# A hybrid recurrence and sparse-attention block: operands of the matrix multiplications moved by 64 bytes in on-chip memory

## The chip, the cores and the metric

The kernel runs on one core of one Trainium2 chip. The time is that of the whole program on the device, in microseconds (us). Before the change three runs took 1340.19, 1340.39 and 1341.03 us; the median, 1340.39 us, is the time that the change is measured against.

TensorE (PE in the profile) multiplies matrices. Each of its products has two operands in the on-chip memory SBUF: a *stationary* one of 128 x 128 elements, which a weight load (PEld, LDWEIGHTS) brings into the array, and a *moving* one of 128 rows and 128 to 512 columns, which then streams through it. Results go to PSUM. VectorE (DVE) and ScalarE (ACT) work on tiles, GpSimd (POOL) does little here, and SyncE (SP) issues nearly all the transfers.

## What is computed

One layer over 512 tokens of width 2048, in float32: a normalisation, one wide projection `w_in`, two branches (a gated linear recurrence, and sparse attention for which an indexer picks the keys), a gated merge, an output projection `w_out`, a residual sum and a last normalisation.

```python
h = rmsnorm(x, norm_w[layer])
proj = h @ w_in[layer]
...
q_idx = (cq @ w_qidx).reshape(b_, s_, IDX_HEADS, IDX_DIM)
kv = (rmsnorm(c_kv, kv_norm_w) @ w_ukv).reshape(b_, s_, B_HEADS, 2 * B_HEAD_DIM)
...
rel_scores = jax.nn.relu(jnp.einsum('bthd,bsd->bths', qi_blk.astype(F32), k_idx))
...
merged = (jax.nn.sigmoid(m_a) * (y_a @ w_pa[layer])
          + jax.nn.sigmoid(m_b) * (y_b @ w_pb[layer]))
x = x + merged @ w_out[layer]
return rmsnorm(x, final_norm_w)
```

## The kernel before

**Three products for one.** A float32 operand is split into a high part that the fast format `fp32r` holds exactly and a low rest (`split`, line 70). `mm3` (line 74) multiplies high by high, high by low and low by high; its three matmuls are lines 75, 76 and 77 of the profile. In the profile's names, `pp<-sh,wh` is a matmul into the PSUM tile `pp` with the moving operand `sh` and the stationary operand `wh`.

**Jobs.** The program is a list of jobs that are run in order. Each takes weights from device memory through two buffers (`load`), has ACT and DVE split them (`prep`, three pieces ahead), and multiplies. Other work (normalisations, the recurrence, attention) is cut into steps, one of which is issued between pieces of a job (`pump`). The order of every engine's instructions is written out this way; no scheduler moves them.

**Units of seven products.** For the gates and for most of the output projection, 2 x 2 blocks of matrices are multiplied with seven block products in place of eight (`pair_unit`, line 1141; `PRODUCTS`, line 1131). A unit has eight *chunks* k = 0 to 7, one for 256 rows of the contracted side; a chunk is 7 products x 2 halves x 3 matmuls = 42 matmuls, each with a moving operand of 256 columns. Thirteen units belong to `w_in` (eleven of `gate_pair` and two more; the moving operand is x: the tiles `xh`, `xl`, and its block sums `sh0` to `sh7` and `sl0` to `sl7`; the stationary one is the weights: `bh`, `bl` as loaded and `wh`, `wl` for the sums that `pair_sums` makes of them). Three more belong to `w_out` (`out_job`, line 1407), where the sides are exchanged: the weights move, and the merged activations (`mh`, `ml`, `so`) are stationary.

**Where operands lie.** Tiles are placed by pools in the order in which they are asked for, so a tile's byte address is settled by what was allocated ahead of it. Here only the address modulo 128 is of interest, called the *residue* below; the operands that this change touches lie at residue 0 or 64. The kernel sets it in several places by spare elements of 4 bytes: `weight_places` (line 136) takes 64 elements more than it needs and starts at `at`; `STILL` and `RANK` are 16 elements, `MOVED` is 48, so all three mean residue 64 and `at` = 0 means residue 0. `pair_specs` (line 1133) has an argument `even`: in the chunk whose number it is, `pair_sums` puts its sums at residue 0 instead of at `R.at`, residue 64.

What the built program places, by the residue of its tiles:

| operands (moving / stationary) | before | after |
|---|---|---|
| units of `w_in`: x and its sums / weights and their sums | 0 / 64, but 64 / 64 for the sums of chunk 2 | 0 / 64, but 0 / 0 for the sums of chunk 2 of the first unit |
| units of `w_out`: weights and their sums / activations | 64 / 0, but 0 / 0 for the sums of chunk 2 of each unit | 64 / 0, but 0 / 0 for the sums of chunk 0 of the first unit |
| index jobs, `w_qidx`, 384 columns: normalised `cqh`, `cql` / weights | 64 / 0 | 64 / 0 in the even jobs, 64 / 64 in the odd ones |
| index scores, 512, 384 and 256 columns: keys `kih`, `kil` / queries `qih`, `qil` | 64 / 64 | 64 / 0 |
| `w_ukv` jobs 1 and 3, keys part, 512 columns: `ckh`, `ckl` / weights | 0 / 0 | 0 / 64 |
| `w_ukv` jobs 1 and 3, values part, 256 columns: weights / `ckh`, `ckl` | 0 / 0 | 64 / 0 |

**Around the index.** Eight jobs over `w_qidx` (line 1238) make the queries of two of the 16 heads each; `qidx_evac` splits them into `qih` and `qil`, and `idx_gen` (line 610) multiplies them with the keys in three sizes and adds what comes out into the score `M`. Its tile `relu` has two buffers and lies above the queries in a pool that grows downwards, so that eight elements more in each of them put the queries 64 bytes lower. Four jobs `ukv_job` (line 932) make keys and values for two heads each.

Of the kernel before, what the change touches and what calls it, by code (L numbers as in the profile page):

```python
# [26 lines left out]
F32 = mybir.dt.float32  # L27
# [8 lines left out]
NK = D // 128  # L36
# [7 lines left out]
STILL, MOVED, RANK = 16, 48, 16  # L44

EVEN = 2
# [4 lines left out]
def hybrid_block(ctx, tc, x, w_in, w_uq, w_qidx, w_ukv, w_pa, w_pb, w_out, rel_bias, final_norm_w,  # L51
# [4 lines left out]
    w_in, w_uq, w_qidx, w_ukv = w_in[0], w_uq[0], w_qidx[0], w_ukv[0]  # L56
    w_pa, w_pb, w_out = w_pa[0], w_pb[0], w_out[0]
# [21 lines left out]
    def mm(ps, l, r, first, last):  # L79
        PE.matmul(ps, l, r, start=first, stop=last, skip_group_check=True)  # L80
# [4 lines left out]
    cols = const.tile([128, 32], F32, name="cols")  # L85
# [11 lines left out]
    gate_d = dram.tile([48, 128, T], F32, name="gate_d")  # L97
# [18 lines left out]
    R = SimpleNamespace(load=0.0)  # L116


    specs = []
# [139 lines left out]
    def start():  # L259
        R.v0 = enter("v0")  # L260
        R.x = enter("sums")
        p0 = enter("p0", side="right")
        R.xt = []
        for k in range(8):
            if k in (EVEN, EVEN + 1):
                R.x.tile([128, STILL if k == EVEN else 64 - STILL], F32, name=f"gap{k}")
            R.xt.append(R.x.tile([128, 2, T], F32, name=f"xt{k}", tag=f"sh{k}"))
            if k < 6:
                xs_l.append(R.x.tile([128, 4, 256], FR, name=f"sl{k}", tag=f"sl{k}"))
            else:  # L270
                R.dg = R.x.tile([128, 1024], F32, name=f"dg{k}", tag=f"sl{k}")
                if k == 6:
                    R.row, R.total = R.dg[:, 0:T], R.dg[:, T:]
        R.rinv = cols[:, 25:29]
        ident = R.dg[:, 0:128]
        parts = ((0, 2), (2, 4), (4, 8), (8, 12), (12, 16))
        wh, wl, wr = [], [], []
        sums = p0.tile([128, 2, T], F32, name="sums")

        def load_x(k, i=None):  # L280
            n = slice(0, 2) if i is None else slice(i, i + 1)
            SP.dma_start(R.xt[k][:, n, :], x_t[:, 2 * k + n.start:2 * k + n.stop, :])

        def load_w(c):
            k0, k1 = parts[c]
            wr.append(p0.tile([128, 4, 272], F32, name="fr", bufs=3))
            SP.dma_start(wr[c][:, 0:k1 - k0, :], w_first[:, k0:k1, :])

        A.dma_start(wc, w_norm)
        load_x(0, 0)  # L290
        load_w(0)
        load_x(0, 1)
        load_w(1)
        load_x(1)
        A.dma_start(ident, c_ident)
        A.dma_start(cols[:, 0:25], w_cols)

        def load_group(c):
            load_x(2 * c - 2)
            load_w(c)  # L300
            load_x(2 * c - 1)

        load_group(2)
        heat_src = p0.tile([128, 128], F32, name="rows")
        G.memset(heat_src, 1.0)
        G.tensor_copy(ones_r, heat_src)
        A.activation(R.rinv[:, 0:1], eps, AF.Sqrt)
        warm = mmp.tile([128, T], F32, name="acc")
        for _ in range(8):
            PE.matmul(warm[:, 0:128], ones, ones, start=True, stop=True)  # L310
        pools4 = [(mmp, "acc"), (sdp, "sd")] * 2
        accs = [pool.tile([128, T], F32, name="pf", tag=tag)[:, 0:272] for pool, tag in pools4]
        squares = {}

        def square(k):
            squares[k] = p0.tile([128, 2, T], F32, name="sq", bufs=3)
            A.activation(squares[k], R.xt[k], AF.Square)

        def add(k):
            if k:  # L320
                V.tensor_tensor(sums, squares.pop(0) if k == 1 else sums, squares.pop(k), op=OP.add)

        def three(c, n):
            k0, k1 = parts[c]
            xp, wp = ((xh, wh), (xl, wh), (xh, wl))[n]
            for k in range(k0, k1):
                for t in range(4):
                    mm(accs[t], xp[k // 4][:, k % 4, t * 128:t * 128 + 128], wp[c][:, k - k0, :],
                       k + n == 0, k == NK - 1 and n == 2)

        behind = ()
        for c, (k0, k1) in enumerate(parts):
            n = slice(0, k1 - k0)
            wh.append(p0.tile([128, 4, 272], FR, name="fh", bufs=3))
            wl.append(p0.tile([128, 4, 272], FR, name="fl", bufs=3))
            G.tensor_copy(wh[c][:, n], wr[c][:, n])
            for k in range(k0, k1):
                src = R.xt[k // 2][:, k % 2, :]
                hi, lo = xh[k // 4][:, k % 4, :], xl[k // 4][:, k % 4, :]
                A.activation(hi, src, AF.Copy, scale=wc[:, k:k + 1])  # L340
                V.scalar_tensor_tensor(lo, src, wc[:, k:k + 1], hi.bitcast(F32), op0=OP.mult, op1=OP.subtract)
            V.tensor_tensor(wl[c][:, n], wr[c][:, n], wh[c][:, n].bitcast(F32), op=OP.subtract)
            if c < 2:
                load_group(c + 3)
            if c == 2:
                load_ahead()
            if c == 4:
                prep(0, 1)
            pairs = range(k0 // 2, k1 // 2)
            for k in behind:  # L350
                square(k)
            for k in behind if c < 4 else ():
                add(k)
            if c == 4:
                last = behind
            behind = pairs
            for n in range(3):
                three(c, n)
        prep(0, 2)
        for k in last:  # L360
            add(k)
        for k in behind:
            square(k)
            add(k)
        V.tensor_tensor(R.total, sums[:, 0, :], sums[:, 1, :], op=OP.add)
        R.first = accs
        leave("p0")
# [232 lines left out]
    def qidx_evac(h0):  # L600
        def evac(c, ps):
            qh = R.q.tile([128, 384], FR, name="qih", bufs=3)
            ql = R.q.tile([128, 384], FR, name="qil", bufs=3)
            split(qh, ql, ps)
            if len(waiting) > 1:
                lanes["misc"].append(waiting.pop(0))
            waiting.append(idx_gen(h0 + c, qh, ql))
        return evac

    def idx_gen(h, qh, ql):  # L610
        place = {b: bank("sc")[:, 0:b * 128 + 128] for b in (3, 2, 1)}
        for b in (3, 2, 1):
            s = slice(b * 128 - 128, b * 128)
            n = slice(0, b * 128 + 128)
            mm3(place[b], qh[:, s], ql[:, s], R.kih[:, n], R.kil[:, n], True, True)
        r = R.q.tile([128, 1280], F32, name="relu", bufs=2)
        for b in (3, 2, 1):
            m = slice(MO[b], MO[b] + b * 128 + 128)
            A.activation(r[:, m], place[b], AF.Relu, scale=IDX_SCALE)
        for b in (3, 2, 1):  # L620
            m = slice(MO[b], MO[b] + b * 128 + 128)
            w = widx[:, b, h:h + 1]
            if h == 0:
                V.tensor_scalar(R.M[:, m], r[:, m], w, None, op0=OP.mult)
            else:
                V.scalar_tensor_tensor(R.M[:, m], r[:, m], w, R.M[:, m], op0=OP.mult, op1=OP.add)
        yield
# [303 lines left out]

    def ukv_job(p):
        at = len(specs)
        specs.append(([(0, 512, w_ukv[0:256, p * 512:(p + 1) * 512])], 2, 512))

        def run():
            drain("att")
# [195 lines left out]
    def pair_specs(src, cols, n, even=-1):  # L1133

        for k in range(n):
            parts = [(i * 256, i * 256 + 256, src[k * 256:(k + 1) * 256, c:c + 256]) for i, c in enumerate(cols)]
            if cols[1] == cols[0] + 256:
                parts = [(0, 512, src[k * 256:(k + 1) * 256, cols[0]:cols[0] + 512])]
            specs.append((parts, 2, 512, "pair", k == even))
# [18 lines left out]
            if k in ahead:  # L1158
                ahead[k]()

    def pair_job(src, cols, n, rhs, evac):
        at = len(specs)
        pair_specs(src, cols, n)
        jobs.append(lambda: pair_unit(at, n, rhs, evac))

    def pair_evac(dst, fn):
# [19 lines left out]
    def gate_pair(j):  # L1186
        fn = AF.Silu if j < 16 else AF.Sigmoid
        pair_job(w_in, [GATE_COL[j], GATE_COL[j] + 256], NK // 2, x_pair,
                 pair_evac([gate_d[j:j + 2], gate_d[j + 2:j + 4]], [fn, fn]))


    GATE_COL = [3072 + j * 128 for j in range(8)] + [5008 + j * 128 for j in range(8)]
# [44 lines left out]
    jobs.append(open_branches)  # L1237
    for p in range(8):
        feat_job(w_qidx, p * 256, 2, 4, 4, lambda k: (R.cqh[:, k, 128:], R.cql[:, k, 128:]),
                 qidx_evac(2 * p), width=384)  # L1240

    def end_index():
        lanes["misc"].extend(waiting)
# [163 lines left out]
    def out_job():  # L1407
        at = len(specs)
        for cb in range(3):
            pair_specs(w_out, [cb * 512, cb * 512 + 256], NK // 2, even=EVEN)  # L1410
        for i in range(8):
            specs.append(([(0, 512, w_out[i * 256:(i + 1) * 256, 1536:])], 2, 512)
                         + ((f"so{i}",) if i >= 4 else ()))
# [217 lines left out]
```

## Time and profile before

| | before |
|---|---|
| median of three runs | 1340.39 us |
| the profiled execution, first to last instruction | 1338.4 us |
| what a run's time has beside that span | 2.0 us |
| PE, busy share of the span | 99% |
| DVE, busy share | 80% |
| ACT, busy share | 50% |
| mean granted PE clock | 0.998 |
| the sixteen units of seven products, matmuls in the trace | 5376 of 10876 |

The time of the profiled execution is known as its span; the 2.0 us is the difference of the runs' median from it. A matmul's row in the profile shows some 0.28 us for 256 columns and 0.39 us for 512, while the next one starts after 0.11 and 0.23 us: matmuls are pipelined, and what one costs is the time from its start to the next one's start. The timeline gives starts to 0.01 us; over many matmuls in a row their count gives the mean to a fraction of a nanosecond.

### The profile page before, as it was taken

The page shows a single profiled execution, that of the slowest core. Times are in us where ns is not written, and L with a number is a line of the kernel's source. Part 1 is how long each engine was busy: PE and PEld are TensorE (multiplying, and loading weights), DVE is VectorE, ACT ScalarE, POOL GpSimd, SP SyncE. Part 2 cuts the span into 40 slices and gives each one's busy share as a digit, 9 for nine tenths or more (in the row PEclk, how much of TensorE's full clock was granted, in tenths as well). Part 3 has the DMA queues.
Part 4 walks back from the last instruction along what each step waited for, and adds up shares of the span by engine and source line. Part 5 has one row for each costly group of instructions (what it writes and reads, how often), then busy time and mean ns, then how long its engine had stood idle before and what let it go on. Part 6 is the DMA issues. An engine that isn't in the chain of part 4 may idle for free.

```text
span 1338.4 us, 26561 instructions
## 1 busy us (share of the span) xinstructions
PE 1327.9 (99%) x10876; PEld 1236.6 (92%) x10876; DVE 1068.6 (80%) x1705; ACT 666.8 (50%) x1060; POOL 39.0 (3%) x54
## 2 busy tenths in 40 slices
PE   9999999999999999999999999999999999999997
PEld 8988999999999999999999888888888888899996
DVE  7777889998888888886778988875656658899856
ACT  6455555454454444443666465656434423444435
POOL 2000000000000000000000000020001000000000
PEclk9999999999999999999999999999999999999999
DMA  6343545543454444434523525445655556653454
GB/s 243 93 112 113 155 142 158 148 141 107 143 158 143 142 143 142 128 113 159 181 85 110 182 73 158 127 149 178 242 193 189 186 177 220 201 162 123 168 202 166
DMA packets 141290, 205.82 MB, mean 154 GB/s; under 512 B 8672, under 2 KB 82032, under 8 KB 141040
## 3 DMA queue, kind: packets, MB, share of 16 engines
q1 hardware_dynamic: 140592, 203.78, 48.3%
q8 instruction: 85, 1.39, 0.4%
q10 hardware_dynamic: 576, 0.35, 0.1%
q14 instruction: 37, 0.30, 0.1%
HBM read 168.42 MB, written 35.68 MB: 152 GB/s over the span
## 4 chain that ended last, share of the span: by engine, by line
PE 96%; DMA 1%; DVE 1%; ACT 1%; SPq 0%; issue 0%; ACTq 0%; DVEq 0%
PE pp L75 15%; PE pp L77 15%; PE pp L76 15%; PE acc L75 14%; PE acc L76 14%; PE acc L77 14%; PE hl L80 1%; PE ho L80 1%; DMA wr<-in_w_in_dram 1%; PE sc L75 1%; PE sc L76 1%; PE sc L77 1%; DMA xt<-in_x_t_dram 0%; PE hp L80 0%; PE po L77 0%; PE po L76 0%
## 5 line engine op out<-in xcount | busy, mean ns | idle before, releaser
L150 ACT ACTIVATE bh<-wr 128x768 fp32r<-128x768 f32 x128 | 108.2, 845 | 215.3 <-issue 99.7
L152 ACT ACTIVATE wh<-sv 128x512 fp32r<-128x512 f32 x256 | 152.3, 623 | 84.4 <-DVE sv L145 66.9
L75 PE MATMUL pp<-sh,wh 128*128 128x256 f32 x624 | 172.7, 277 | 0.0
L77 PE MATMUL pp<-sh,wl 128*128 128x256 f32 x624 | 172.7, 277 | 0.0
L76 PE MATMUL pp<-sl,wh 128*128 128x256 f32 x624 | 172.6, 277 | 0.0
L72 DVE TENSOR_TENSOR wl<-wr,wh 128x1024 fp32r<-128x1024 f32 (+1 forms) x104 | 125.6, 1209 | 56.7 <-ACT wh L71 56.7
L154 DVE TENSOR_TENSOR wl<-sv,wh 128x1024 fp32r<-128x1024 f32 x128 | 156.5, 1222 | 6.1
L153 DVE TENSOR_TENSOR bl<-wr,bh 128x768 fp32r<-128x768 f32 x128 | 122.2, 955 | 46.9 <-ACT bh L150 46.2
L71 ACT ACTIVATE wh<-wr 128x1024 fp32r<-128x1024 f32 (+1 forms) x104 | 108.2, 1040 | 92.2 <-PE acc L76 44.1
L75 PE MATMUL acc<-xh,wh 128*128 128x512 f32 x304 | 120.3, 396 | 0.0
L76 PE MATMUL acc<-xl,wh 128*128 128x512 f32 x304 | 118.5, 390 | 0.0
L77 PE MATMUL acc<-xh,wl 128*128 128x512 f32 x304 | 118.5, 390 | 0.0
L76 PEld LDWEIGHTS pp<-sl,wh 128*128 128x128 f32 x624 | 117.3, 188 | 0.0
L75 PEld LDWEIGHTS pp<-sh,wh 128*128 128x128 f32 x624 | 117.3, 188 | 0.0
L77 PEld LDWEIGHTS pp<-sh,wl 128*128 128x128 f32 x624 | 117.3, 188 | 0.0
L75 PE MATMUL pp<-xh,bh 128*128 128x256 f32 x416 | 114.8, 276 | 0.0
L77 PE MATMUL pp<-xh,bl 128*128 128x256 f32 x416 | 114.8, 276 | 0.0
L76 PE MATMUL pp<-xl,bh 128*128 128x256 f32 x416 | 114.8, 276 | 0.0
L75 PE MATMUL acc<-yh,wh 128*128 128x512 f32 x256 | 100.3, 392 | 0.0
L76 PE MATMUL acc<-yl,wh 128*128 128x512 f32 x256 | 99.7, 390 | 0.0
L77 PE MATMUL acc<-yh,wl 128*128 128x512 f32 x256 | 99.7, 389 | 0.0
L145 DVE TENSOR_TENSOR sv<-wr 128x512 f32<-128x512 f32 x128 | 87.9, 686 | 7.2 <-DMA wr<-in_w_in_dram 4.4
(390 smaller groups left out, 3608.4 us busy)
## 6 DMA issues: line engine op xcount, KB each, us to landing
wr<-in_w_in_dram SPq DMA_DIRECT2D x136, 512.0 KB, 3.8
wr<-in_w_out_dram SPq DMA_DIRECT2D x32, 512.0 KB, 3.8
mg<-gate_d SPq DMA_DIRECT2D x48, 256.0 KB, 4.2
gate_d<-c SPq DMA_DIRECT2D x44, 256.0 KB, 4.9
wr<-in_w_in_dram SPq DMA_DIRECT2D x36, 256.0 KB, 3.0
wr<-in_w_pa_dram SPq DMA_DIRECT2D x16, 512.0 KB, 4.3
wr<-in_w_pb_dram SPq DMA_DIRECT2D x16, 512.0 KB, 4.1
wr<-in_w_qidx_dram SPq DMA_DIRECT2D x8, 512.0 KB, 4.1
```

The source lines that it names most:

```text
L71: A.activation(hi, src, AF.Copy)
L72: V.tensor_tensor(lo, src, hi.bitcast(F32), op=OP.subtract)
L75: PE.matmul(ps, lh, rh, start=first, stop=False, skip_group_check=True)
L76: PE.matmul(ps, lh, rl, start=False, stop=False, skip_group_check=True)
L77: PE.matmul(ps, ll, rh, start=False, stop=last, skip_group_check=True)
L80: PE.matmul(ps, l, r, start=first, stop=last, skip_group_check=True)
L145: V.tensor_tensor(sv[:, 0:2, :], b[:, 1:3, :], b[:, 0:1, :].to_broadcast([128, 2, 256]), op=OP.add)
L150: A.activation(bh, b[:, 1:4, :], AF.Copy)
L152: A.activation(vh[:, i:i + 2, :], sv[:, i:i + 2, :], AF.Copy)
L153: V.tensor_tensor(bl, b[:, 1:4, :], bh.bitcast(F32), op=OP.subtract)
L154: V.tensor_tensor(vl, sv, vh.bitcast(F32), op=OP.subtract)
```

## The change

Four edits, none of which adds, removes or reorders an instruction: on each engine the instructions stand as they stood, apart from the numbers of buffers and lines.

- `start` no longer allocates two gaps of 16 and 48 elements before the tiles `xt2` and `xt3` (whose places the sums `sh2`, `sl2` and `sh3` take later), so that all of x's sums lie at residue 0.
- The argument `even`, which puts the weight sums of one chunk at residue 0, is given to the first unit of `w_in` alone (chunk 2), and of `w_out` to the first unit alone, where it is now chunk 0.
- The tile `relu` is 1288 elements wide in place of 1280.
- The odd jobs of `w_ukv` and of `w_qidx` have their weights at residue 64 instead of 0.

```diff
@@ start
         for k in range(8):
-            if k in (EVEN, EVEN + 1):
-                R.x.tile([128, STILL if k == EVEN else 64 - STILL], F32, name=f"gap{k}")
             R.xt.append(R.x.tile([128, 2, T], F32, name=f"xt{k}", tag=f"sh{k}"))
@@ idx_gen
-        r = R.q.tile([128, 1280], F32, name="relu", bufs=2)
+        r = R.q.tile([128, 1288], F32, name="relu", bufs=2)
@@ ukv_job
-        specs.append(([(0, 512, w_ukv[0:256, p * 512:(p + 1) * 512])], 2, 512))
+        specs.append(([(0, 512, w_ukv[0:256, p * 512:(p + 1) * 512])], 2, 512, RANK if p % 2 else 0))
@@ pair_job
-    def pair_job(src, cols, n, rhs, evac):
+    def pair_job(src, cols, n, rhs, evac, even=-1):
         at = len(specs)
-        pair_specs(src, cols, n)
+        pair_specs(src, cols, n, even)
@@ gate_pair
-                 pair_evac([gate_d[j:j + 2], gate_d[j + 2:j + 4]], [fn, fn]))
+                 pair_evac([gate_d[j:j + 2], gate_d[j + 2:j + 4]], [fn, fn]), even=EVEN if j == 0 else -1)
@@ the eight index jobs
         feat_job(w_qidx, p * 256, 2, 4, 4, lambda k: (R.cqh[:, k, 128:], R.cql[:, k, 128:]),
-                 qidx_evac(2 * p), width=384)
+                 qidx_evac(2 * p), width=384, place=RANK if p % 2 else 0)
@@ out_job
-            pair_specs(w_out, [cb * 512, cb * 512 + 256], NK // 2, even=EVEN)
+            pair_specs(w_out, [cb * 512, cb * 512 + 256], NK // 2, even=-1 if cb else 0)
```

## The prediction

> **What bounds the kernel now.** I read the page first (busy times, the granted clock in slices, the chain of work that ended last), then the list of all that PE waited for.
>
> ```profile
> PE 1327.9 (99%) x10876; PEld 1236.6 (92%) x10876; DVE 1068.6 (80%) x1705; ACT 666.8 (50%) x1060; POOL 39.0 (3%) x54
> PEclk9999999999999999999999999999999999999999
> PE 96%; DMA 1%; DVE 1%; ACT 1%; SPq 0%; issue 0%; ACTq 0%; DVEq 0%
> PE acc L310 <- POOL ones_r L306: 1.4, 1, 1.4
> PE pf L80 <- ACT xh L340: 0.6, 1, 0.6
> PE pf L80 <- POOL fh L336: 0.3, 1, 0.3
> PE pf L80 <- DVE fl L342: 0.3, 1, 0.3
> ```
>
> PE is the bound, at full clock, and waits 2.6 us in all, at the very start. So the time can only fall if matmuls start closer to each other, and a nanosecond per matmul is worth about 11 us over the 10876. Busy time says nothing on that, since rows overlap; I therefore took starts from the timeline of PE. The first matmul (L75) of a chunk is easy to find, and a chunk is 42 matmuls. In the sixth of the `w_in` units, chunk 2, chunk 3 and chunk 4 begin at the first three rows here, and chunk 2 of the next unit at the fourth:
>
> ```profile
> 334.22 0.28 PE L75 MATMUL pp<-xh,bh 128*128 128x256 f32 x1
> 339.14 0.28 PE L75 MATMUL pp<-xh,bh 128*128 128x256 f32 x1
> 343.90 0.28 PE L75 MATMUL pp<-xh,bh 128*128 128x256 f32 x1
> 372.46 0.28 PE L75 MATMUL pp<-xh,bh 128*128 128x256 f32 x1
> ```
>
> Chunk 2 takes 4.92 us, chunk 3 takes 4.76, and the six chunks from 343.90 on take 28.56, again 4.76 each: 113.3 ns per matmul. Chunk 2 is the one in which x's sums share residue 64 with the weights. What would meet there is shown by two more rows:
>
> ```profile
> 145.44 0.28 PE L75 MATMUL pp<-sh,wh 128*128 128x256 f32 x1
> 145.44 0.19 PEld L76 LDWEIGHTS pp<-sl,wh 128*128 128x128 f32 x1
> ```
>
> The weight load for the next matmul begins with the matmul itself, so one stationary and one moving operand are read from SBUF together. My reading, an inference from which chunks are long: equal residues cost, unequal ones do not. Only 24 of the 42 matmuls of chunk 2 have equal residues, so 0.16 us is 6.7 ns for each.
>
> The output units tell a second thing. The first matmuls of chunks 0 to 4 of the first unit, then of chunks 2, 3 and 4 of the second, and of the third:
>
> ```profile
> 1170.77 0.28 PE L75 MATMUL pp<-bh,mh 128*128 128x256 f32 x1
> 1175.71 0.28 PE L75 MATMUL pp<-bh,mh 128*128 128x256 f32 x1
> 1180.66 0.28 PE L75 MATMUL pp<-bh,mh 128*128 128x256 f32 x1
> 1185.63 0.28 PE L75 MATMUL pp<-bh,mh 128*128 128x256 f32 x1
> 1190.40 0.28 PE L75 MATMUL pp<-bh,mh 128*128 128x256 f32 x1
> 1218.96 0.28 PE L75 MATMUL pp<-bh,mh 128*128 128x256 f32 x1
> 1223.87 0.28 PE L75 MATMUL pp<-bh,mh 128*128 128x256 f32 x1
> 1228.64 0.28 PE L75 MATMUL pp<-bh,mh 128*128 128x256 f32 x1
> 1257.20 0.28 PE L75 MATMUL pp<-bh,mh 128*128 128x256 f32 x1
> 1262.11 0.28 PE L75 MATMUL pp<-bh,mh 128*128 128x256 f32 x1
> 1266.88 0.28 PE L75 MATMUL pp<-bh,mh 128*128 128x256 f32 x1
> ```
>
> Chunks 0 and 1 of the first unit take 4.94 and 4.95 us (118 ns per matmul) although their residues are unequal; chunk 2, with equal ones, takes 4.97; chunk 3 takes 4.77, and from then on a chunk with unequal residues takes 4.76. So a stream of 256-column matmuls has two steady spacings, loose (118) and tight (113.3), keeps the one it has, and a stretch of equal residues leaves it in the tight one. That is what the one odd chunk per unit buys, and why the change keeps one, placed earlier here.
>
> **The change part by part.** No instruction moves; each term is a number of matmuls by a change of their distance. All lie on PE, so all move the end, if nothing takes PE's place. DVE is the next busiest:
>
> ```profile
> 148.00:181.00 33.00, 33.00 (x293) 33.00 (x293) 27.65 (x41) 16.76 (x27) 0.00 (x0) 1.00 0.36 110
> 1313.82 0.76 DVE L1515 TENSOR_TENSOR o<-acc,o 128x256 f32<-128x256 f32 x2 [1.35 <-PE acc L77]
> ```
>
> In this stretch of a `w_in` unit (columns: PE, PEld, DVE, ACT and POOL busy) DVE needs 27.65 of 33.00 us, and a unit becomes 0.4% shorter: it keeps up. At the end DVE waits 1.35 us for PE before the last chain begins; its work ahead of that is paced by the same PE stream and comes earlier too. If that cover were gone, at most what arrives too early would be lost.
>
> *`w_in`*: twelve of thirteen units lose their long chunk, 12 x 0.16 = **-1.92 us**. The first keeps one, at residues 0 / 0 in place of 64 / 64; the output's chunk 2 shows that 0 / 0 costs the same, so 0. The bounds: -1.92 if the tight spacing lasts, and for the other end see rival C.
>
> *`w_out`*: the first unit's chunks 0 to 3 took 19.63 us (1170.77 to 1190.40). With the odd chunk first they should take 4.97, 4.77, 4.76 and 4.76 = 19.26: -0.37. The second and third unit lose (4.91 + 4.77) - 2 x 4.76 = 0.16 each. Together **-0.69**. If the stretch in chunk 0 does not bring the tight spacing, all 24 chunks stay at 4.95: 118.8 against now 19.63 + 20 x 4.76 + 0.32 = 115.15, so +3.6. I take -0.69, since chunk 2 starts from the same loose spacing now.
>
> *Keys and values*: job 1 of `w_ukv` begins its keys part, its values part and ends at
>
> ```profile
> 939.42 0.44 PE L75 MATMUL acc<-ckh,wh 128*128 128x512 f32 x1
> 942.23 0.28 PE L75 MATMUL acc<-wh,ckh 128*128 128x256 f32 x1
> 945.11 0.40 PE L75 MATMUL acc<-yh,wh 128*128 128x512 f32 x1
> ```
>
> The values part, equal residues, is 24 matmuls in 2.88 us, 120 ns each. Unequal, they go to 113.3 or 118: two jobs, -0.32 to -0.10; I take **-0.2**, the middle, as either spacing may be entered. The keys part (512 columns) goes from equal to unequal. For long runs of 512 columns with equal residues:
>
> ```profile
> 91.38 0.39 PE L75 MATMUL acc<-xh,wh 128*128 128x512 f32 x1
> 93.42 0.39 PE L75 MATMUL acc<-xh,wh 128*128 128x512 f32 x1
> ```
>
> Nine in 2.04 us, 227 ns. No long run with unequal residues exists. The keys part takes 2.81 us where 12 x 0.227 = 2.72; two jobs: -0.2 to +0.2, taken as 0.
>
> *Index scores*: in the rows below the scores of one head begin at 636.87 (512 columns), 637.57 (384), 638.11 (256) and end at 638.47.
>
> ```profile
> 636.87 0.40 PE L75 MATMUL sc<-kih,qih 128*128 128x512 f32 x1
> 637.57 0.34 PE L75 MATMUL sc<-kih,qih 128*128 128x384 f32 x1
> 638.11 0.28 PE L75 MATMUL sc<-kih,qih 128*128 128x256 f32 x1
> 638.47 0.33 PE L75 MATMUL acc<-cqh,wh 128*128 128x384 f32 x1
> 638.98 0.34 PE L75 MATMUL acc<-cqh,wh 128*128 128x384 f32 x1
> 640.37 0.34 PE L77 MATMUL acc<-cqh,wl 128*128 128x384 f32 x1
> 640.55 0.40 PE L75 MATMUL sc<-kih,qih 128*128 128x512 f32 x1
> ```
>
> That is 0.70 + 0.54 + 0.36 = 1.60 us at equal residues. With every matmul at its best seen pace, 3 x 0.227 + 3 x 0.174 + 3 x 0.113 = 1.54: 16 heads x 0.06 = -0.96. But the sizes change every three matmuls, so no steady spacing is reached; the bounds are -0.96 and +0.1 (nothing gained, rounding), and I take about half, **-0.5**.
>
> *Odd index jobs*: 4 jobs x 24 = 96 matmuls of 384 columns go from unequal to equal. Unequal, they take (640.37 - 638.98) / 8 = 0.174. Equal at 384 columns is only seen in single steps: 0.54 / 3 = 0.18 among the scores, and 0.18 for the last one ahead of them. The 512-column stream stands at its pace with equal residues, which speaks for no cost. Bounds: 96 x 6.7 ns = +0.64 (the price at 256 columns), and -0.3, if equal residues let them run 3 ns closer, as the first after the scores do (638.47 to 638.98, 0.17 each). I take **+0.35**, by the 0.18 rows, which are nearest in size.
>
> Last, the spacing that the index leaves behind: the 47 matmuls from
>
> ```profile
> 689.38 0.28 PE L75 MATMUL acc<-wh,xh 128*128 128x256 f32 x1
> 694.91 0.28 PE L77 MATMUL acc<-wh,xl 128*128 128x256 f32 x1
> ```
>
> take 5.53 us, 118 ns each, the loose spacing. They may be entered at the tight one: 47 x 4.4 ns, -0.2 or 0; I take 0.
>
> The sum: -1.92 - 0.69 - 0.2 - 0.5 + 0.35 = -2.96 us. The profiled execution's span would be 1335.4 instead of 1338.4; the 2.0 us by which the runs' median exceeds that span is taken as unchanged: 1340.39 - 2.96 = **1337.4 us**.
>
> **The rivals.**
>
> *A, the index takes back more.* Scores gain nothing, odd jobs pay the full 0.64: -1.92 - 0.69 - 0.1 + 0.64 = -2.1, so 1338.3 us, within what counts as no change. For it: short sequences never reach a steady spacing. Against: 120 ns is seen only at equal residues.
>
> *B, every term at its good end.* -1.92 - 0.69 - 0.32 - 0.96 + 0 - 0.2 = -4.1: 1336.3 us.
>
> *C, the tight spacing is lost.* Now each unit renews it in chunk 2; then only the first unit does. Were it lost at some unit's start (in the evacuation and the next unit's first weights), every later `w_in` chunk would cost 4.946 - 4.76 = 0.19 us more. The other terms save 2.96, so it decides from about 16 loose chunks: lost before the eleventh unit's end, the kernel is slower. Lost half-way (48 chunks): 1337.4 + 9.1 = 1346.5 us. For it: the loose spacing of 1170.77 did not mend itself in 84 matmuls. Against: the six chunks from 343.90 to 372.46 cross the boundary of two units at 4.76 each, and PE has no wait there that could upset it.
>
> *D, nothing.* The long chunks would be long for another reason than residues (what ACT, DVE or a transfer do just then), and removing equal residues would change nothing: 1340.4 us. Against: in both kinds of units the long stretch is where the residues are equal, though in one it is x that was moved and in the other the weights. The Trainium skill, "SBUF — State Buffer", section "Who interferes with whom", holds that PE's two read ports, for the moving operand and for weight loads, are independent, and that PE never waits on anyone. By that rule the sum would be 0 and the time 1340.4; the 4.92 against 4.76 us of two neighbouring chunks does not agree with it.
>
> **How the numbers follow.** Chances: the forecast 0.61, A 0.21, B 0.08, C 0.05, D 0.05. The range 1336.2 to 1338.9 holds the forecast, A and B with a little for the runs' own spread (0.84 us before). A measurement of this kernel tells about 0.2% from no change, 2.7 us: the border is 1337.7, close above the forecast. Of its cases I put three quarters on the faster side (0.46), with B 0.54; the rest, A and D are 0.41 as no change; slower is C, 0.05.
>
> **What would show it.** All `w_in` chunks after the first unit's chunk 2 at 4.76 us; in the output, chunk 0 of the first unit at 4.97, then 4.77, then 4.76 to the end; a head's scores near 1.57; an odd index job's first run of twelve near 2.13 in place of 2.08; the values parts of jobs 1 and 3 at 2.72 or 2.83. A `w_in` chunk at 4.95 after some unit's start would be C, a chunk of 4.92 that is still there would be D.

## The result, and the profile after

The changed kernel takes 1356.70 us, median of four runs (1356.39 to 1357.20); the kernel before took 1340.43 beside them (1340.19 to 1341.03). The ratio is 1.0121, with a 95% interval of 1.0108 to 1.0133: 16.3 us slower. The forecast was 1337.4, faster.

The page of the changed kernel, its busy times, granted clock and chain, and the costliest PE group in the list by shapes (columns: count, busy us, mean ns of one, idle us before):

```profile
span 1355.4 us, 26563 instructions
PE 1345.4 (99%) x10876; PEld 1254.6 (93%) x10876; DVE 1068.2 (79%) x1705; ACT 666.8 (49%) x1060; POOL 35.5 (3%) x54
PEclk9999999999999999999999999999999999999999
PE 98%; DVE 1%; ACT 1%; DMA 0%; issue 0%; SPq 0%; ACTq 0%
L75 PE MATMUL pp<-sh,wh 128*128 128x256 f32 x624 | 175.4, 281 | 0.0
```

The same group in the list of the kernel before:

```profile
L75 PE MATMUL pp<-sh,wh 128*128 128x256 f32 x624 | 172.7, 277 | 0.0
```

The same engine, the same number of matmuls, the same clock, no new wait, and 17.0 us more of span. The matmuls of the `w_in` units have become longer: 281 ns where they had 277. The timeline of PE says where. The first matmuls of chunks 1, 2, 3 and 4 of the first `w_in` unit, of the last chunk of the thirteenth, and of the job behind it:

```profile
139.28 0.28 PE L75 MATMUL pp<-xh,bh 128*128 128x256 f32 x1
144.04 0.28 PE L75 MATMUL pp<-xh,bh 128*128 128x256 f32 x1
148.99 0.28 PE L75 MATMUL pp<-xh,bh 128*128 128x256 f32 x1
153.93 0.28 PE L75 MATMUL pp<-xh,bh 128*128 128x256 f32 x1
643.65 0.28 PE L75 MATMUL pp<-xh,bh 128*128 128x256 f32 x1
648.60 0.34 PE L75 MATMUL acc<-cqh,wh 128*128 128x384 f32 x1
```

Chunk 1 takes 4.76 us, the tight spacing (113.3 ns per matmul). Chunk 2, which has the one stretch of equal residues that the change keeps, takes 4.95 (4.94 by the nanoseconds of the trace), and from 148.99 to 648.60 there are 101 chunks in 499.61 us: 4.947 each, the loose spacing (117.8 ns per matmul), to the end of the stage. From the start of the first unit to the end of the last, `w_in` takes 514.2 us in place of 497.3: **+17.0 us**. In `w_out` the first unit's chunks 0, 1, 2 and 3 begin at the first four rows, the second unit at the fifth, the last chunk of the third at the sixth:

```profile
1188.50 0.28 PE L75 MATMUL pp<-bh,mh 128*128 128x256 f32 x1
1193.47 0.28 PE L75 MATMUL pp<-bh,mh 128*128 128x256 f32 x1
1198.25 0.28 PE L75 MATMUL pp<-bh,mh 128*128 128x256 f32 x1
1203.01 0.28 PE L75 MATMUL pp<-bh,mh 128*128 128x256 f32 x1
1226.81 0.28 PE L75 MATMUL pp<-bh,mh 128*128 128x256 f32 x1
1298.21 0.28 PE L75 MATMUL pp<-bh,mh 128*128 128x256 f32 x1
```

4.97, then 4.78 (4.773 by the trace), then 4.76 each: what was forecast, -0.69 us. So one stage did the reverse of what it was to do, and nearly all of the result lies in it. The rest of the span's 17.0 us is small: +1.0 ahead of the first unit (which begins anywhere from 132.8 to 134.4 us in the profiles of this study), -0.5 in the index jobs, and +0.2 spread between the index and the merge.

### The profile page after: what moved, and what is told of

The parts are those of the page before. It is cut to its first block, busy times and chain, and to the rows that moved or that the text cites. A ratio compares the mean times of both kernels' runs of the same rounds, so it can differ in the third digit from the quotient of the medians.

```text
span 1355.4 us, 26563 instructions
## 1 busy us (share of the span) xinstructions
PE 1345.4 (99%) x10876; PEld 1254.6 (93%) x10876; DVE 1068.2 (79%) x1705; ACT 666.8 (49%) x1060; POOL 35.5 (3%) x54
## 4 chain that ended last, share of the span: by engine, by line
PE 98%; DVE 1%; ACT 1%; DMA 0%; issue 0%; SPq 0%; ACTq 0%
PE pp L76 16%; PE pp L77 15%; PE pp L75 15%; PE acc L75 14%; PE acc L76 14%; PE acc L77 14%; PE pf L80 2%; PE hl L80 1%; PE ho L80 1%; PE sc L76 1%; PE sc L75 1%; PE sc L77 1%; PE hp L80 0%; PE po L77 0%; PE po L76 0%; PE po L75 0%
```

## Experiments

In what follows 64 / 64 and 0 / 0 give the residue of the moving operand and then that of the stationary one. The theory formed from the profile after, called S: the stretch of equal residues in `w_in` is itself what sets the loose spacing. A spacing, once set, stays; and which one a stretch sets depends on how it is made. Before the change the sums of x, the moving operand, were laid on the weights' residue (64 / 64). Now the weights' sums, the stationary operand, are laid on x's (0 / 0). The rivals: the tight spacing does not last if it is not renewed in each unit (R), or the new places of x's sums are at fault (P).

**The stretch in `w_in` taken away.** In the changed kernel:

```diff
-                 pair_evac([gate_d[j:j + 2], gate_d[j + 2:j + 4]], [fn, fn]), even=EVEN if j == 0 else -1)
+                 pair_evac([gate_d[j:j + 2], gate_d[j + 2:j + 4]], [fn, fn]))
```

> The changed kernel without its one stretch of equal residues in w_in: all 13 units have unequal residues in every chunk. Theory S (the stretch itself, which moves the stationary operand's residue, sets the loose spacing; without it the tight spacing that chunk 1 has anyway lasts): chunks 1 to 103 take 4.76 us each, the time is about 1337.1 us (1340.4 - 1.92 - 0.16 in w_in, -0.69 in w_out, about -0.5 around the index). Theory R (the tight spacing does not last unless each unit renews it): some unit falls back to 4.95 us per chunk and stays there; between 1338 and 1356 us by where. Theory P (the new places of x's sums, 64 and 256 bytes lower, are what is loose, with or without a stretch): 4.95 us from chunk 2 or 3 on, about 1356 us.

Measured: six runs, of which four took 1336.66 to 1337.58 us and two took 1356.17 and 1356.26. Over all six the ratio to the kernel before is 1.0022, with an interval of 0.9975 to 1.0069: no difference is shown. The profile is of one of the first kind. Its chunk 1, chunk 2, last chunk and the end of the stage:

```profile
137.80 0.28 PE L75 MATMUL pp<-xh,bh 128*128 128x256 f32 x1
142.56 0.28 PE L75 MATMUL pp<-xh,bh 128*128 128x256 f32 x1
623.32 0.28 PE L75 MATMUL pp<-xh,bh 128*128 128x256 f32 x1
628.08 0.33 PE L75 MATMUL acc<-cqh,wh 128*128 128x384 f32 x1
```

From 137.80 to 628.08 are 103 chunks of 4.76 us: 4326 matmuls without a renewal, and the tight spacing holds to the end. That is against R, and, since the places of x's sums are the new ones, against P. But the two runs at 1356.2 are 19.1 us above the others, and 103 chunks by 0.187 are 19.3. No profile was taken of them, but their times fit a `w_in` that was loose from its first chunks on. So without a stretch the spacing is left to chance, which none of the three theories had said.

**Both kinds of stretch in one kernel.** The changed kernel with the gaps ahead of x's sums put back, so that chunk 2 of every `w_in` unit has 64 / 64 as before the change, and the 0 / 0 of the first unit moved to its chunk 4:

```diff
+            if k in (EVEN, EVEN + 1):
+                R.x.tile([128, STILL if k == EVEN else 64 - STILL], F32, name=f"gap{k}")
             R.xt.append(R.x.tile([128, 2, T], F32, name=f"xt{k}", tag=f"sh{k}"))
...
-  even=EVEN if j == 0 else -1)
+  even=4 if j == 0 else -1)
```

> The changed kernel with the gaps before x's sums put back, so that every w_in unit has in chunk 2 a stretch in which the moving operand's residue changes (64 / 64, as before the change), and the first unit has besides, in chunk 4, one in which the stationary operand's changes (0 / 0). Theory S: chunks 5, 6, 7 of the first unit and 0, 1 of the second take 4.95 us, chunk 2 of the second unit brings 4.76 back, all later ones are as before the change; about 1340.4 us (5 x 0.19 and 0.2 for chunk 4 lost, 0.69 and 0.5 gained elsewhere). Theories R and P: no chunk at 4.95, since each unit renews the tight spacing and the places are the old ones; about 1339.4 us.

Measured: 1340.83 us, one run. The first matmuls of chunks 1 to 5 of the first unit, and of chunks 2, 3 and 4 of the second:

```profile
138.47 0.28 PE L75 MATMUL pp<-xh,bh 128*128 128x256 f32 x1
143.42 0.28 PE L75 MATMUL pp<-xh,bh 128*128 128x256 f32 x1
148.41 0.28 PE L75 MATMUL pp<-xh,bh 128*128 128x256 f32 x1
153.17 0.28 PE L75 MATMUL pp<-xh,bh 128*128 128x256 f32 x1
158.11 0.28 PE L75 MATMUL pp<-xh,bh 128*128 128x256 f32 x1
182.84 0.28 PE L75 MATMUL pp<-xh,bh 128*128 128x256 f32 x1
187.83 0.28 PE L75 MATMUL pp<-xh,bh 128*128 128x256 f32 x1
192.59 0.28 PE L75 MATMUL pp<-xh,bh 128*128 128x256 f32 x1
```

Chunk 1 is loose this time (4.95). The stretch at 64 / 64 in chunk 2 (4.99) leaves chunk 3 tight (4.76). The one at 0 / 0 in chunk 4 (4.94) leaves the five chunks from 158.11 to 182.84 loose (24.73 us, 4.946 each). The next one at 64 / 64 (4.99) brings 4.76 back. Each kind set its own spacing against the other within 50 us, in the same stage of one execution: S holds for `w_in`, R and P fall. The loose start was expected by none of the theories; of the 0.4 us over the forecast, 0.3 is its price.

**The fourth combination, in `w_out`.** Is it the moved operand that matters? In `w_out` the activations are stationary. The kernel without a stretch in `w_in`, with the activations' sums of chunk 4 at residue 64, made 64 / 64 by the stationary operand (the tile `wk` that takes the place later is widened to match, at residue 0; not shown):

```diff
-        sums = pool.tile([128, 2, 4, 256], FR, name=f"so{k}", tag=tag)
+        if k == 4:
+            sums = pool.tile([128, 2080], FR, name=f"so{k}", tag=tag)[:, 16:2064].rearrange(
+                "p (i b n) -> p i b n", i=2, b=4)
+        else:
+            sums = pool.tile([128, 2, 4, 256], FR, name=f"so{k}", tag=tag)
```

> As the kernel without a stretch in w_in, and in w_out the activations' sums of chunk 4 (stationary there) lie at residue 64, so that each output unit has in chunk 4 a stretch of equal residues 64 / 64 made by the stationary operand. Theory S in its general form (a stretch made by moving the moving operand leaves the tight spacing, one made by the stationary operand the loose one, whichever residue they meet on): from chunk 5 of the first output unit on all chunks but the chunks 4 are at 4.95 us, 17 x 0.19 + about 0.4 for the chunks 4 more than without: about 1340.6 us if w_in stays tight. If what is loose after a stretch depends on the residue 0 / 0 in w_in alone: the chunks after it stay at 4.76, about 0.5 us more: 1337.6 us.

Measured: 1337.43 us, one run. Chunks 4, 5 and 6 of the first output unit:

```profile
1187.47 0.28 PE L75 MATMUL pp<-bh,mh 128*128 128x256 f32 x1
1192.37 0.28 PE L75 MATMUL pp<-bh,mh 128*128 128x256 f32 x1
1197.13 0.28 PE L75 MATMUL pp<-bh,mh 128*128 128x256 f32 x1
```

Chunk 4 takes 4.90, chunk 5 is tight, and so are all later ones outside the chunks 4. S in its general form, by which operand is moved, is wrong. This run left open whether that stretch sets the tight spacing or only keeps it, so it was put alone: the same kernel without the weights' stretch in chunk 0 (`even=-1` in all of `w_out`).

> As the kernel without a stretch in w_in; in w_out the stretch of the weights' sums (0 / 0) is gone and the one by the activations' sums in chunk 4 (64 / 64, stationary) is alone. The output's first unit starts loose: chunks 0 to 3 at 4.95 us. If the stationary stretch at 64 / 64 sets the tight spacing by itself, chunks 5 to 7 and the later units are at 4.76; if it only keeps what it finds, all stay at 4.95 (20 x 0.19 = 3.8 us more).

Measured: 1338.65 us, one run. Chunks 3, 4, 5 and 6 of the first output unit:

```profile
1183.70 0.28 PE L75 MATMUL pp<-bh,mh 128*128 128x256 f32 x1
1188.65 0.28 PE L75 MATMUL pp<-bh,mh 128*128 128x256 f32 x1
1193.60 0.28 PE L75 MATMUL pp<-bh,mh 128*128 128x256 f32 x1
1198.36 0.28 PE L75 MATMUL pp<-bh,mh 128*128 128x256 f32 x1
```

Chunk 3 is loose (4.95; so were chunks 0 to 2), chunk 4 is the stretch (4.95), chunk 5 is tight (4.76), and so is the rest. It sets the spacing by itself. So the four combinations stand like this; only one of them sets the loose spacing:

| moving / stationary around it | the stretch | made by | what follows | seen in |
|---|---|---|---|---|
| 0 / 64 (`w_in`) | 64 / 64 | moving | tight | before, and the run with both |
| 0 / 64 (`w_in`) | 0 / 0 | stationary | **loose** | after, and the run with both |
| 64 / 0 (`w_out`) | 0 / 0 | moving | tight | before, after |
| 64 / 0 (`w_out`) | 64 / 64 | stationary | tight | the two runs above |

In each row the stretch sets the spacing against the other one in at least one profile. For the first row that is the run with both stretches, and two of the runs below, where chunk 1 was loose and chunk 3 is tight; in the profile before, chunk 1 was tight already.

In `w_in` the two kinds also differ in which of a chunk's seven products have equal residues: the third to the sixth by x's sums, the third to the fifth and the seventh by the weights' sums. That does not explain the difference. The 0 / 0 of `w_out` has the same products as the 0 / 0 of `w_in`, and by the nanoseconds of the changed kernel's trace PE settles at 113 to 114 ns behind both of its parts there, and at 117 to 119 in `w_in`.

**The part in `w_out` alone.** The kernel before, with the one edit `even=-1 if cb else 0` in `out_job`.

> The kernel before with one part of the change: in w_out the stretch stands in chunk 0 of the first unit alone. Theory S and all others: chunk 0 of the first output unit 4.97 us, chunk 1 4.77, all 22 later ones 4.76; 0.69 us less than before, 1339.7 us. If the tight spacing needs renewal in w_out, the second or third unit falls back to 4.95 per chunk: up to 1342.7.

Measured: 1339.41 us, median of four runs (1339.34 to 1339.61); ratio 0.9992, interval 0.9979 to 1.0005, which does not tell it from no change. The trace does: chunks 0, 1 and 2, and the end of the third unit:

```profile
1170.66 0.28 PE L75 MATMUL pp<-bh,mh 128*128 128x256 f32 x1
1175.63 0.28 PE L75 MATMUL pp<-bh,mh 128*128 128x256 f32 x1
1180.41 0.28 PE L75 MATMUL pp<-bh,mh 128*128 128x256 f32 x1
1285.13 0.39 PE L75 MATMUL acc<-wh,mh 128*128 128x512 f32 x1
```

4.97, 4.78, then 22 chunks in 104.72, 4.76 each: the term of -0.69 as worked out.

**The index queries alone.** The kernel before, with `relu` 1288 wide and nothing else.

> The kernel before with one edit, relu 1288 wide, so the index queries lie at residue 0. If the scores' gain of 0.53 us is theirs alone, the nine matmuls of a head take 1.56 us in place of 1.59 and the twelve of 384 columns 2.08 in every job; about 1339.9 us.

Measured: 1340.77 us, one run. By the trace a head's nine score matmuls take 1.559 to 1.567 us in place of 1.594, and the scores in all 24.97 us in place of 25.48; the changed kernel has 24.95. The gain of 0.5 us is the queries' alone. The time is 0.9 us over the expected one all the same: this run had a loose start in `w_in` (chunk 1 at 4.95), which costs 0.3, and a wait of 0.4 us in the recurrence, for which the profile shows no cause.

**The stretch that was wanted, once.** If a stretch at 64 / 64 is what is needed, the first unit can have one without a place of its own for x's sums: they are copied once to where `cqh` and `cql` are kept later, at residue 64. The kernel without a stretch in `w_in`, with this (K is 1 here, and `x_first` is used by the first unit alone):

```diff
             split(xs_h[k], xs_l[k], d)
+            if k == K:
+                R.kept = [a.rearrange("p a t -> p (a t)")[:, 0:1024].rearrange("p (i n) -> p i n", i=4)
+                          for a in (R.cqh, R.cql)]
+                A.activation(R.kept[0], xs_h[k].bitcast(F32), AF.Copy)
+                V.tensor_copy(R.kept[1], xs_l[k].bitcast(F32))
...
+    def x_first(k):
+        out = x_pair(k)
+        if k == K:
+            out = [o[:3] + [a[:, i, :] for i in range(4)] for o, a in zip(out, R.kept)]
+        return out
```

> The changed kernel with another stretch in w_in: the first unit takes the block sums of its chunk 1 from copies at residue 64 (in the place where cqh and cql are kept later), so that the moving operand meets the weights at 64 / 64 there, once; no other chunk of w_in has equal residues. Theory S, now: in w_in a stretch at 64 / 64 leaves the tight spacing whatever was there before, one at 0 / 0 leaves the loose one, and without a stretch it is settled by a stall of some 20 to 40 ns in chunk 0, which differs from run to run. Then chunk 1 takes 4.92 to 4.99 us, every later one 4.76, in every run: 1337.2 to 1337.6 us, and no run near 1356. If what was seen is chance in each run and not the stretch, some of the runs are near 1356.

Measured: 1338.66 us, median of eleven runs (1337.66 to 1341.64), none near 1356; ratio 0.9987, interval 0.9978 to 0.9996. The spacing is as forecast: in the profile chunk 1 takes 4.92 and every later one 4.76. But chunk 0 ends tight in this profile, so it shows the spacing kept; that the stretch sets it rests on the eleven times. Most of the 1.1 us over the forecast is in chunk 0, 5.82 us in place of 4.92: PE waits there once more, as its list of waits shows.

```profile
PE pp L75 <- ACT c L490: 0.7, 1, 0.7
```

ACT's copy `c` takes a result of the job ahead out of PSUM, and the unit's fifth product is written to the same buffer. ACT begins it at 136.35 us, in place of 135.46 in the kernel before; why it was later was not followed up. The same with the copies for chunk 0, which are made earlier (K is 0):

> The same with the copies and the stretch at 64 / 64 in chunk 0 of the first unit, where the stall is. Theory S: 11 matmuls of equal residues follow the stall and set the tight spacing, so chunk 1 is already at 4.76; 1337.0 to 1337.4 us in every run. If a stretch has to be longer than that after a stall, some runs are near 1356.

Measured: **1337.47 us**, median of eleven runs (1336.83 to 1339.40), none near 1356; ratio 0.9978, interval 0.9969 to 0.9987. Chunks 0, 1 and 2, the last chunk and the end of the stage:

```profile
133.61 0.28 PE L75 MATMUL pp<-xh,bh 128*128 128x256 f32 x1
138.59 0.28 PE L75 MATMUL pp<-xh,bh 128*128 128x256 f32 x1
143.35 0.28 PE L75 MATMUL pp<-xh,bh 128*128 128x256 f32 x1
624.11 0.28 PE L75 MATMUL pp<-xh,bh 128*128 128x256 f32 x1
628.87 0.33 PE L75 MATMUL acc<-cqh,wh 128*128 128x384 f32 x1
```

4.98, then 103 chunks in 490.28, 4.76 each; by the nanoseconds of the trace PE comes into this stretch at 118 and leaves it at 113. Not every run lies in the expected 1337.0 to 1337.4 us; the highest, 1339.40, was not followed up. The median is 2.95 us below that of the kernel before, and 19 below that of the changed kernel: the forecast's time, reached with the other stretch. Without a stretch two runs of six took some 1356 us; with either of these, none of 22.

## Why the prediction was wrong

*The bound, and what a nanosecond per matmul is worth.* Right. PE has no new wait and the clock is the same; the loss came from 4.4 ns in each of some 4200 matmuls.

*Two spacings, kept until something sets them.* Right, and more lasting than could be known: 4326 matmuls in a row.

*"A stretch of equal residues leaves it in the tight one."* This step failed. It was drawn from two combinations, 64 / 64 in `w_in` and 0 / 0 in `w_out`, and used for a third, 0 / 0 in `w_in`, of which the profile before has no row. The sentence that carried it was that the first unit's stretch is now "at residues 0 / 0 in place of 64 / 64; the output's chunk 2 shows that 0 / 0 costs the same, so 0". The stretch did cost the same, 4.94 us. What it left behind was not the same: 101 chunks by 0.187 us, +18.9, against the -1.92 of the term, whose chunks it would otherwise have shortened. Equal residues had been looked at as a pair of numbers, without what lies around them. Why 0 / 0 inside 0 / 64 leaves the loose spacing stays open.

*Rival C.* It had the price per chunk, and the shape (lost once, never mended), and a time of 1346.5 us for a loss half-way; with the loss in the first unit its own working gives 1337.4 + 101 x 0.19 = 1356.6 us. Its cause was wrong: no boundary between units upsets the spacing. It got 0.05, since the boundaries looked harmless, and they are. The danger lay in the edit that was costed at nothing.

*The first unit.* The prediction did not ask why chunk 1 was tight in the profile before. It differs from one execution to the next (below).

*`w_out`*: -0.69 forecast, -0.69 by the trace, and again alone. *Scores*: -0.5 forecast, -0.53 (25.48 to 24.95 us). *Odd index jobs*: +0.35 forecast, +0.05 (33.28 to 33.33 us in all the index jobs): runs of 384 columns go to 173 ns at equal residues as well. The 0.18 rows, by which the term was sized, do not carry over to such runs. Nor were they steps between sizes: in the changed kernel the scores change size as before, at unequal residues, and their steps of 384 columns take 173 to 175 ns in place of about 180. The prediction's "no steady spacing is reached" was too strong for these. *Values*: -0.2 forecast, -0.09 (2.872 to 2.828 us in each of two jobs), the loose spacing. *Keys*: 0 forecast, +0.07 (2.817 to 2.852 us each). The 47 matmuls behind the index stayed loose, as taken. Rival B is called "every term at its good end" but takes the odd jobs at 0, where their bound was -0.3; that changed nothing in the outcome.

*Rival D*, by which residues mean nothing to PE, is refuted: the chunks 2 of the later units went from 4.92 to 4.76 us in the kernel without a stretch, and the rule of the Trainium skill ("SBUF — State Buffer", section "Who interferes with whom") that was put beside it, that PE never waits on anyone, does not cover what was seen.

## What to carry to other kernels

Where an engine is always busy and waits for nothing, look at the distance from start to start and not at durations: three spacings of one and the same matmul, 113.3, 117.8 and 120 ns, stood beside each other here, and a whole stage can sit in the wrong one. A piece of work that seems only to cost something may set the pace of all that follows, so what is to replace it wants a row of its own, in the same surroundings. A pace that is settled at the start of a stage, differently from run to run, shows only over several runs: without its stretch in `w_in` this kernel took 1337 us in four and 1356 in two.

## What the runs showed of the hardware

*How the addresses of the two operands lie to each other sets the spacing.* In streams of 256 columns in `fp32r` a matmul takes 120 ns where the addresses are equal modulo 128 bytes, and 113.3 or 117.8 where they differ by 64; other residues were not tried. The stretch that the activations make in `w_out` is less regular: 118.3 ns on average in the first of its two runs, with steps from 112 to 123. Runs of 384 columns take 173 ns at equal and at unequal residues, and long runs of 512 columns 227 at equal ones. That the load of the next stationary operand and the read of the moving one get in each other's way is a reading of this and is not shown.

*Without a stretch, the spacing of `w_in` is settled in its first chunk.* Every profile begins the first unit loose. In the eight in which nothing else sets the spacing of chunk 1, the step from the 25th to the 26th matmul is longer than the 118 ns ahead of it, and a few matmuls behind it PE is tight or loose. By the nanoseconds of the trace that step was 150, 152, 134, 151 and 146 ns where chunk 1 was tight (before, after, no stretch in `w_in`, and the two with a stationary stretch in `w_out`), and 149, 147 and 135 where it was loose (both stretches, `w_out` alone, `relu` alone). The length of this stall does not order them, and what does is not known. Two rows each, of the kernel without a stretch (134, then tight) and of the one with both (149, then loose):

```profile
135.73 0.30 PE L75 MATMUL pp<-sh,wh 128*128 128x256 f32 x1
135.86 0.28 PE L76 MATMUL pp<-sl,wh 128*128 128x256 f32 x1
```

```profile
136.33 0.31 PE L75 MATMUL pp<-sh,wh 128*128 128x256 f32 x1
136.47 0.28 PE L76 MATMUL pp<-sl,wh 128*128 128x256 f32 x1
```

In the kernel before, the chunk 2 of each unit hides this: whatever the start, the stage is tight from chunk 3 of its first unit on.

*What stays open*: why 0 / 0 inside 0 / 64 leaves the loose spacing and the other three combinations the tight one, and what decides at the stall in the first chunk. The trace shows starts, not reads of SBUF, and the mirrored case for x, weights at 0 and x at 64 in `w_in`, was not tried.
